# The spatial branch's products as three float16 products of scaled halves, in place of float32 products

## The chip, the cores and the metric

The kernel runs on one core of one Trainium2 chip. The metric is the device time in microseconds (us) of one execution of the whole program; a profiled execution adds a trace of each engine's instructions, whose span runs from the first to the last of them. A core has the engines TensorE (PE, matrix products, with its weight loads PEld), VectorE (DVE), ScalarE (ACT) and GpSimd (POOL), which share the on-chip memory SBUF; products land in the eight banks of PSUM. SyncE (SP), ACT and POOL also issue transfers (DMA).

## The reference

One step of a model layer with three token mixers, for 2048 sample tokens and 128 prompt tokens (2176 together, 17 chunks of 128), with a model width of 1024 and a branch width of 512. From the normalised tokens one input projection gives the columns of branch A (a gated delta rule), branch B (spatial gating in chunks), branch C (a Fourier transform) and the merge gates. The branches are projected, gated, summed and projected again. The change lies in branch B:

```
vn = rmsnorm(v, g_norm).reshape(B, n, CHUNK_B, G_B, CH_B)
vs = jnp.einsum('gpq,bnqgc->bnpgc', w_s, vn) + b_s.T[None, None, :, :, None]
return u * vs.reshape(B, T, W_BR)
```

Here CHUNK_B = 128, G_B = 4 and CH_B = 128: in each chunk of 128 tokens and each of 4 groups of 128 channels, a 128x128 matrix `w_s[g]` mixes the tokens. The root-mean-square is taken over all 512 channels of a token. `u` and the gate `z` of the branch come from the same input projection. All inputs and outputs are float32.

## The kernel before

**Splitting.** Nearly every product is done as three float16 products: an operand is scaled by a power of two, its high half is the float16 of that, and its low half is the float16 of what is left. `mm3` (L168) adds high x high, high x low and low x high in one PSUM bank. `scales` (L183) finds a power of two from a sum of squares: a product with ones adds over the partitions, and three integer operations on DVE make the scale and its inverse. Weights are converted so in `converting` (L203), by an ACT square with a running sum, `scales`, an ACT copy to float16 (L223) and a DVE operation for the low half (L224). The spatial products were an exception: they are float32 (`mm` at L1164).

**Order of the work.** The main line of the program is a sequence of stages: the modulation and the normalised tokens `xh`, `xl`; the columns of branch A with their short convolution (L611); the spatial branch's `v` (L1175); its `u` and `z` (L1207); branch C (L1242); the merges with the gates (L1356); the output projection (L1507). Beside it runs a second line, the delta rule of branch A (`prep`, `base_inverse`, `scan`), as a generator that `pace` (L312) advances a step whenever the main line has done a certain amount of work (`pace.tick`). So both lines are in one program. The tile framework then orders the instructions of each engine ahead of time with a simulated timeline (`schedule_with_timeline_sim=True`, L1572); blocks under `tc.high_priority()` go ahead there. On the chip each engine runs its own queue in that fixed order.

**Around the change.** `wsn`, the four matrices, is loaded at L638 into a buffer of the tag "st" (three buffers). Before the loop TensorE transposes them into a PSUM bank of `ps_x` (two banks) and DVE copies that to `wsT`, float32 (L1156). The loop at L1175 takes the 17 chunks of 128 tokens. For each, TensorE adds 8 x 3 float16 products of 128x512 into a bank of `ps_mm` (three banks); DVE scales it into `vn` (L1184, tag "sg", four buffers); ACT squares it with a sum over the 512 channels (L1187, its output in "st" is not used); DVE and POOL make the reciprocal root (L175, L176). Then `spatial` runs for the chunk before (L1160): four float32 products, stationary `vn`, moving `wsT`, and four DVE operations that multiply by the gain and add the bias (L1166). Results are stored to DRAM up to three chunks later (`vstore`, L1169). Last in the body, DVE multiplies `vn` by the root (L1193), for the next turn's `spatial`, and `pace.tick(5.2)` advances the delta rule.

The stage after it reads the results back by channel group (`vrow`, L1206 and L1212) and multiplies them by `u` straight from PSUM (L1218); `z` goes through a sigmoid on ACT (L1128) and a DVE product (L1130). Both take banks of `ps_mm`.

The delta rule's work beside this stage is the preparation of its chunks (L686: transposes L695 and L728, squares L701, roots L702 and L703, DVE products L743 and L759, halves L747 and L748) and the inverses of 32x32 triangles (L771: the ladder on DVE at L792 and L793, halves at L798 and L799).

Of the kernel before, what the change touches and what calls it, by code (L numbers as in the profile page):

```python
# [11 lines left out]
F16 = mybir.dt.float16  # L12
I32 = mybir.dt.int32
BF16 = mybir.dt.bfloat16
AF = mybir.ActivationFunctionType
ALU = mybir.AluOpType
# [4 lines left out]
P = 128  # L21
# [7 lines left out]
WB = 512  # L29
EPS = 1e-6  # L30
# [5 lines left out]
AD = (0, 2, 4, 6)  # L36
CQ = 545
FS = 4096.0
TBS = [(0, 512), (512, 512), (1024, 512), (1536, 512), (2048, 128)]

_CONSTS = [
# [75 lines left out]
def hybrid_flow_kernel(ctx: ExitStack, tc: tile.TileContext, x_prompt, x_sample, state_delta, c, c_ctx, ln_g, w_ada,  # L117
# [3 lines left out]
    V, A, G, PE, SY = nc.vector, nc.scalar, nc.gpsimd, nc.tensor, nc.sync  # L121
    uid, rot = [0], [0]

    def nm(s):
        uid[0] += 1
        return f"{s}_{uid[0]}"
# [4 lines left out]
    def sb(pl, shape, tag, dt=F32, bufs=None):  # L131
        kw = {} if bufs is None else {"bufs": bufs}
        return pl.tile(list(shape), dt, tag=tag, name=nm(tag), **kw)
# [9 lines left out]
    ep = pool(ctx, "ep", 2)  # L143
# [18 lines left out]
    mhalf = sb(cp, [P, 1], "mhalf")  # L162
    G.memset(mhalf, -0.5)

    def mm(out, l, r, start=True, stop=True):
        PE.matmul(out, l, r, start=start, stop=stop)  # L166

    def mm3(out, l, r, start=True, stop=True):  # L168

        mm(out, l[0], r[0], start, False)  # L170
        mm(out, l[0], r[1], False, False)
        mm(out, l[1], r[0], False, stop)

    def rsqrt(out, ss, mul, w):
        V.tensor_scalar(out, ss, mul, EPS, ALU.mult, ALU.add)  # L175
        G.tensor_tensor(out, out, mhalf.to_broadcast([P, w]), ALU.pow)  # L176
# [6 lines left out]
    def scales(ss, pl, tag, sb16=None):  # L183

        ps = bank(ps_x, [P, 1])
        mm(ps, ones16, widened(ss, pl, tag) if sb16 is None else sb16)
        t = sb(pl, [P, 4], tag)
        V.tensor_copy(t[:, 0:1], ps)
        h = t[:, 3:4].bitcast(I32)
        V.tensor_scalar(h, t[:, 0:1].bitcast(I32), 24, None, ALU.logical_shift_right)  # L190
        V.tensor_scalar(t[:, 1:2].bitcast(I32), h, -8388608.0, 204.0 * 8388608, ALU.mult, ALU.add)
        V.tensor_scalar(t[:, 2:3].bitcast(I32), h, 8388608.0, 50.0 * 8388608, ALU.mult, ALU.add)
        return t[:, 1:2], t[:, 2:3]
# [164 lines left out]
    pc = sb(cp, [P, NPRM], "pc")  # L358
# [9 lines left out]
        V.tensor_copy(pc, pp)  # L368

    convw = lambda j, ct: pc[:, 8 + j * 12 + ct:8 + j * 12 + ct + 1]  # L370
    sgug = lambda g: pc[:, 44 + g:45 + g]
    ong = pc[:, 48:49]


# [22 lines left out]
    for blk in range(8):  # L397
        if blk == XB:
            load_x(*TBS[0])
            columns()  # L400
        ps = bank(ps_d, [2, 256])
        for k0 in range(0, KT, 4):
            st = sb(p0p, [P, 4, 256], "ast", bufs=8)
# [31 lines left out]
    with tc.issue_after(last_ada.ins):  # L435
        read_next()
        read_next()
        load_x(*TBS[1])
        zaw = getw(4)
        bdp = sb(wp, [P, KT, 32], "bdp", F16, bufs=1)  # L440
        bdw = load_w(w_in_[:, C_BD:C_BD + 16], KT, 16, hi=bdp[:, :, 0:16], lo=bdp[:, :, 16:32], tag="d")
    szlate = []
    for ti, (t0, tn) in enumerate(TBS):
        if t0 not in xts:
            load_x(t0, tn)
        g = 0 if t0 < NS else 1
# [10 lines left out]
        for k in range(KT):  # L457
            ps = bank(ps_d, [P, tn])
            for j in range(nt):
                PE.transpose(ps[:, j * P:(j + 1) * P], xt[:, j, k * P:(k + 1) * P], ident)  # L460
            t = sb(p0p, [P, tn], "xm", bufs=3)
# [3 lines left out]
        for g in range(4):  # L465
            ps = bank(ps_d if tn == P and g % 2 else ps_mm, [P, tn])
# [33 lines left out]
    def decays():  # L500
# [14 lines left out]
        for d in range(2):  # L515
            A.activation(beta[:, d], pbv[:, 0, d], AF.Sigmoid, scale=bdw.inv)
        V.tensor_scalar(beta, beta, 1.0 / (FS * FS), None, ALU.mult)
        yield 1
# [40 lines left out]
        A.activation(flat(ed), flat(ed), AF.Exp)  # L559
        V.tensor_scalar(flat(ed), flat(ed), FS, None, ALU.mult)  # L560
        V.tensor_scalar(flat(neg), flat(eg), -1.0 / FS, None, ALU.mult)
        yield 1
# [48 lines left out]
    for ct in range(12):  # L611
        w = getw(1, 2 if ct < 6 else min(4, 15 - ct))
        for half in range(1):
# [3 lines left out]
            G.memset(raw[:, LP - 1:LP], 0.0)  # L617
            for t0, tn in TBS:
                flip[0] ^= 1
                ps = bank(ps_d if flip[0] else ps_mm, [P, tn])  # L620
# [65 lines left out]
    def prep(g, ci, t, nxt, held):  # L686
# [40 lines left out]
        for h in range(H):  # L727
            PE.transpose(ps[:, hs(h)], tok[:, 0, hs(h)], ident)  # L728
        made = A.activation(T[:, 0, :], ps, AF.Copy, scale=FS)
        V.scalar_tensor_tensor(T[:, 1, :], ps, FS, T[:, 0, :], ALU.mult, ALU.subtract)  # L730
        more(2, lambda: rows(2, nxt))
# [8 lines left out]
        for d in range(2):  # L740
# [5 lines left out]
            n16 = sb(d2, [P, 2, WB], "n16", F16, bufs=4)  # L746
            made = A.activation(n16[:, 0, :], n_, AF.Copy, scale=FS)  # L747
            V.scalar_tensor_tensor(n16[:, 1, :], n_, FS, n16[:, 0, :], ALU.mult, ALU.subtract)  # L748
# [373 lines left out]
    def silu_unit(ti, w, out_scale=None):  # L1122
        t0, tn = TBS[ti]
        ps = bank(ps_mm, [P, tn])
# [8 lines left out]
    def gate_unit(n, g, ti, w, src, sg=None, out_scale=None):  # L1133

        t0, tn = TBS[ti]
        own = sg is None
# [11 lines left out]
    bp = pool(bs, "bp", 2)  # L1148
    bsp = sb(bp, [P, 4, P], "bsp", bufs=1)
    SY.dma_start(bsp, b_spatial[0].rearrange("g (o p) -> o g p", o=1).to_broadcast([P, 4, P]))  # L1150
    wsT = sb(bp, [P, 4, P], "wsT", bufs=1)
    vw = getw(4, 3)
    ps = bank(ps_x, [P, 4, P])
    for g in range(4):
        PE.transpose(ps[:, g, :], wsn[:, g, :], ident)
    V.tensor_copy(wsT, ps)  # L1156
    vinv = sb(ep, [P, 4], "vinv", bufs=1)
    for i in range(4):
        V.tensor_copy(vinv[:, i:i + 1], vw[i].inv)
    def spatial(t, vn):  # L1160
        vs = sb(bp, [P, 4, P], "vs", bufs=4)
        ps = bank(ps_x, [P, 4, P])
        for g in range(4):
            mm(ps[:, g, :], vn[:, g, :], wsT[:, g, :])  # L1164
        for g in range(4):
            V.scalar_tensor_tensor(vs[:, g, :], ps[:, g, :], sgug(g), bsp[:, g, :], ALU.mult, ALU.add)  # L1166
        vout.append((t, vs))

    def vstore(made):  # L1169
# [4 lines left out]
    vout, vprev = [], None  # L1174
    for t in range(NCH):  # L1175
        ps = bank(ps_mm, [P, 4, P])
        ts = slice(t * P, (t + 1) * P)
        for k in range(KT):
            mm(ps, xh[:, k, ts], v4[0][:, :, k, :], k == 0, False)
            mm(ps, xh[:, k, ts], v4[1][:, :, k, :], False, False)  # L1180
            mm(ps, xl[:, k, ts], v4[0][:, :, k, :], False, k == KT - 1)
        vn = sb(ep, [P, WB], "sg", bufs=4).rearrange("p (i c) -> p i c", i=4)
        with tc.high_priority():
            V.tensor_tensor(vn, ps, vinv.rearrange("p (i o) -> p i o", o=1).to_broadcast([P, 4, P]), ALU.mult)  # L1184
        sq = sb(ep, [P, WB], "st", bufs=3)
        ss = sb(bp, [P, 1], "vss", bufs=3)
        made = A.activation(sq, vn.rearrange("p i c -> p (i c)"), AF.Square, accum_out=ss)  # L1187
        rsqrt(ss, ss, 1.0 / WB, 1)
        if vprev is not None:
            spatial(*vprev)  # L1190
        if len(vout) > 2:
            vstore(made)
        V.tensor_scalar(vn, vn, ss, None, ALU.mult)  # L1193
        vprev = (t, vn)
        if t == 8:
            SY.dma_start(cf, consts16)
        pace.tick(5.2)
    spatial(*vprev)
    while vout:
        vstore(made)  # L1200
# [6 lines left out]
    for g in range(4):  # L1207
# [5 lines left out]
        for ti, (t0, tn) in enumerate(TBS):  # L1213
            st = vrow[:, t0:t0 + tn]
            ps = bank(ps_mm, [P, tn])
# [26 lines left out]
    for g in range(4):  # L1242
        xw, zw = getw(2, 2)
        for gh in range(1):
# [20 lines left out]
            for q in range(0, NCH, 4):  # L1265
                qn = min(4, NCH - q)
                ps = bank(ps_mm, [P, qn, P])
                for i in range(qn):
                    t = q + i
# [43 lines left out]
            for q4 in range(5):  # L1313
# [8 lines left out]
                if q4 == 2:  # L1322
                    ps = bank(ps_x, [P, P])
# [183 lines left out]
    for i_, t in enumerate(order):  # L1507
# [11 lines left out]
        for i, (c0, c1) in enumerate([(0, 512), (512, 896), (896, D)] if end else [(0, 512), (512, D)]):  # L1519
            cs = slice(c0, c1)  # L1520
            ps = bank(ps_mm, [P, c1 - c0])
# [54 lines left out]
```

## Time and profile before

| what | us |
|---|---|
| timed runs | 2195.5, 2200.12, 2200.22 (median 2200.12) |
| the profiled execution | 2197.38 |
| its span | 2195.6 |
| PE busy in the span | 2122.4 |
| DVE busy | 1311.2 |
| ACT busy | 1013.1 |
| POOL busy | 737.1 |

How to read the profile. Busy time is the union of an engine's instructions; matrix products are pipelined, so their durations overlap and a busy PE isn't at its peak. A row of the timeline gives start, duration, engine, line, operation, what is written and read, shapes and count, and in brackets the idle time of the engine before it with what ended it. A row of the stretches gives the stretch, its length, then for PE, PEld, DVE, ACT and POOL the busy time with the count of instructions, the granted TensorE clock (1.00 is full), the mean share of the DMA engines and GB/s. A row of a line or a tile gives the count, the least, median and greatest duration in ns, and the first and last start in us. A row of the groups gives count, busy us, mean ns, and then the idle time before it and what ended most of it.

### The profile page before, as it was taken

The page shows a single profiled execution, that of the slowest core. Times are in us where ns is not written, and L with a number is a line of the kernel's source. Part 1 is how long each engine was busy: PE and PEld are TensorE (multiplying, and loading weights), DVE is VectorE, ACT ScalarE, POOL GpSimd, SP SyncE. Part 2 cuts the span into 40 slices and gives each one's busy share as a digit, 9 for nine tenths or more (in the row PEclk, how much of TensorE's full clock was granted, in tenths as well). Part 3 has the DMA queues.
Part 4 walks back from the last instruction along what each step waited for, and adds up shares of the span by engine and source line. Part 5 has one row for each costly group of instructions (what it writes and reads, how often), then busy time and mean ns, then how long its engine had stood idle before and what let it go on. Part 6 is the DMA issues. An engine that isn't in the chain of part 4 may idle for free.

```text
span 2195.6 us, 42626 instructions
## 1 busy us (share of the span) xinstructions
PE 2122.4 (97%) x16258; PEld 1218.2 (55%) x16258; DVE 1311.2 (60%) x3141; ACT 1013.1 (46%) x2345; POOL 737.1 (34%) x893
## 2 busy tenths in 40 slices
PE   7999999999999999899899999999999999999998
PEld 3565444455455577777455555555655444444444
DVE  5736845479878697466655555755574544233454
ACT  3544644355555674444544445655553422222332
POOL 1421533223334332443321223345442222122553
PEclk9999999999999999999999999999999999999999
DMA  8434733167777754434645556766665544333542
GB/s 282 143 96 146 266 114 110 61 208 219 239 224 238 213 167 107 119 118 143 217 155 166 167 161 187 239 195 206 204 200 154 166 125 129 119 101 109 183 151 106
DMA packets 304280, 365.11 MB, mean 166 GB/s; under 512 B 39393, under 2 KB 215754, under 8 KB 302026
## 3 DMA queue, kind: packets, MB, share of 16 engines
q1 hardware_dynamic: 251690, 267.38, 40.5%
q0 software_dynamic: 12688, 51.27, 6.5%
q10 hardware_dynamic: 39696, 43.72, 5.9%
q8 instruction: 128, 2.10, 0.4%
q14 instruction: 78, 0.64, 0.1%
HBM read 234.67 MB, written 127.62 MB: 165 GB/s over the span
## 4 chain that ended last, share of the span: by engine, by line
PE 45%; DVE 8%; DMA 7%; ACT 3%; issue 2%; POOL 1%; ACTq 0%; SPq 0%; POOLq 0%; DVEq 0%
PE b L166 45%; DMA st<-br 1%; DMA wst<-in_w_in_dram 1%; DVE XB L792 1%; DVE E L793 1%; DMA ei<-XB 1%; DMA wst<-in_w_branch_dram 1%; DMA sv<-kv 1%; DMA mt<-mrg 1%; DVE wlo L224 1%; DVE o L925 0%; DMA mrg<-mrow 0%; ACT nd L745 0%; DVE sv L980 0%; DVE big L1354 0%
## 5 line engine op out<-in xcount | busy, mean ns | idle before, releaser
L166 PE MATMUL b<-xh,whi 128*128 128x512 f16 (+1 forms) x1920 | 650.2, 347 | 7.4 <-DVE sg L1130 3.4
L166 PE MATMUL b<-xl,whi 128*128 128x512 f16 (+1 forms) x1920 | 650.6, 347 | 0.0
L166 PE MATMUL b<-xh,wlo 128*128 128x512 f16 (+1 forms) x1920 | 649.8, 347 | 0.0
L166 PEld LDWEIGHTS <-whi 128*128 128x128 f16 x3904 | 356.7, 98 | 339.6 <-issue 15.8
L166 PEld LDWEIGHTS <-wlo 128*128 128x128 f16 x1952 | 191.1, 98 | 177.9 <-issue 1.5
L166 PE MATMUL b<-big,bhi 128*128 128x512 f16 (+1 forms) x960 | 251.7, 348 | 5.8 <-ACT big L1353 5.4
L1393 POOL TENSOR_TENSOR mrow<-mrow,sg 128x512 f32<-128x512 f32 (+1 forms) x80 | 96.0, 1201 | 289.0 <-DVE sg L1392 158.5
L166 PE MATMUL b<-big,blo 128*128 128x512 f16 (+1 forms) x480 | 163.7, 348 | 0.0
L1383 ACT ACTIVATE sg<-b,winv 128x512 f32<-128x512 f32 (+1 forms) x120 | 74.1, 618 | 154.0 <-PE b L166 153.6
L166 PEld LDWEIGHTS <-xh 128*128 128x128 f16 x1496 | 118.7, 99 | 35.0 <-DVE yT L1306 3.9
L633 POOL TENSOR_TENSOR cy<-cy,raw 128x545 f32<-128x545 f32 (+1 forms) x48 | 76.6, 1623 | 180.3 <-ACT raw L632 180.3
L166 PEld LDWEIGHTS <-bhi 128*128 128x128 f16 x960 | 87.2, 98 | 77.0 <-ACT big L1353 1.6
L180 DVE CAST wscb<-wss 128x1 bf16<-128x1 f32 x93 | 14.3, 154 | 192.4 <-ACT wlo L214 79.4
L1392 DVE SCALAR_TENSOR_TENSOR sg<-b,binv,sg 128x512 f32<-128x512 f32 (+1 forms) x80 | 53.5, 668 | 101.2 <-PE b L166 91.1
L166 PE MATMUL b<-whi,xh 128*128 128x128 f16 x544 | 95.2, 222 | 5.2 <-DVE yT L1306 3.7
L166 PE MATMUL b<-wlo,xh 128*128 128x128 f16 x544 | 95.2, 222 | 0.0
L166 PE MATMUL b<-whi,xl 128*128 128x128 f16 x544 | 95.1, 222 | 0.0
L166 PE MATMUL b<-wohi,mh 128*128 128x512 f16 (+2 forms) x248 | 91.9, 372 | 1.5 <-ACT mh L1463 1.5
L865 POOL COPY T<-ES 32x256 f16<-32x256 f16 x68 | 28.7, 422 | 191.5 <-DMA ES<-ei 178.2
L166 PE MATMUL b<-wohi,ml 128*128 128x512 f16 (+2 forms) x248 | 91.7, 372 | 0.3 <-DVE ml L1464 0.3
L166 PE MATMUL b<-wolo,mh 128*128 128x512 f16 (+2 forms) x248 | 91.9, 372 | 0.0
L224 DVE SCALAR_TENSOR_TENSOR wlo<-wst,wsc,whi 128x1024 f16<-128x1024 f32 x52 | 72.6, 1399 | 31.2 <-ACT whi L223 30.4
(458 smaller groups left out, 4305.2 us busy)
## 6 DMA issues: line engine op xcount, KB each, us to landing
wst<-in_w_in_dram SPq DMA_DIRECT2D x60, 512.0 KB, 5.9
qkv<-cy POOLq DMA_DIRECT2D x12, 1089.0 KB, 5.2
st<-br SPq DMA_DIRECT2D x48, 256.0 KB, 4.5
mrow<-mrg SPq DMA_DIRECT2D x18, 512.0 KB, 3.5
mrow<-mrg SPq DMA_DIRECT2D x16, 576.0 KB, 3.8
mrg<-mrow POOLq DMA_DIRECT2D x16, 576.0 KB, 3.8
dc<-dec SPq DMA_DIRECT2D x17, 512.0 KB
kq<-qkv SPq DMA_DIRECT2D x34, 256.0 KB, 5.1
```

What stands on the lines that cost most here:

```text
L166: PE.matmul(out, l, r, start=start, stop=stop)
L180: V.tensor_copy(sb16, ss)
L224: V.scalar_tensor_tensor(w.lo, st, s, w.hi, ALU.mult, ALU.subtract)
L633: G.tensor_tensor(y[:, c0:c1], y[:, c0:c1], raw[:, 1 + c0:1 + c1], ALU.mult)
L792: V.tensor_tensor(t3, X3[:, 0:k, k:k + 1].to_broadcast([P, k, n_]), E3[:, k:k + 1, k:32].to_broadcast([P, k, n_]), ALU.mult)
L793: V.tensor_tensor(E3[:, 0:k, k:32], E3[:, 0:k, k:32], t3, ALU.subtract)
L865: G.tensor_copy(T16[rows(a0, b), :, :, b], ES[0:32, :, 2 * a0 + b, :, wT])
L1383: A.activation(sg, ps, AF.Sigmoid, scale=gw.inv)
L1392: V.scalar_tensor_tensor(sg, ps, binv[:, 1:2], sg, ALU.mult, ALU.mult)
L1393: G.tensor_tensor(mr, mr, sg, ALU.add)
```

## The change

The spatial weights are now held as two float16 halves under one scale, which `scales` finds from their sum of squares; its inverse goes into a small tile `vg` with the gains. A chunk's values get a fixed scale of 2048 (`VS`), folded into the reciprocal root's constants; ACT makes the high half from `vn` times the root and DVE the low half, in a buffer of the tag "st", over the square's unused output. `vn` itself is no longer scaled in place. `spatial` calls `mm3` in place of `mm`, and its evictions multiply by `vg` in place of the gain.

```
+VS = 2048.0
...
-    sgug = lambda g: pc[:, 44 + g:45 + g]
...
-    wsT = sb(bp, [P, 4, P], "wsT", bufs=1)
+    wsT = sb(bp, [P, 2, 4, P], "wsT", F16, bufs=1)
     vw = getw(4, 3)
     ps = bank(ps_x, [P, 4, P])
     for g in range(4):
         PE.transpose(ps[:, g, :], wsn[:, g, :], ident)
-    V.tensor_copy(wsT, ps)
+    wss = sb(bp, [P, 1], "vss", bufs=3)
+    A.activation(wsT[:, 1], ps, AF.Square, accum_out=wss)
+    wscale, winv_ = scales(wss, bp, "wssc")
+    A.activation(wsT[:, 0], ps, AF.Copy, scale=wscale)
+    V.scalar_tensor_tensor(wsT[:, 1], ps, wscale, wsT[:, 0], ALU.mult, ALU.subtract)
+    vg = sb(bp, [P, 4], "vg", bufs=1)
+    V.tensor_scalar(vg, pc[:, 44:48], winv_, 1.0 / VS, ALU.mult, ALU.mult)
...
         for g in range(4):
-            mm(ps[:, g, :], vn[:, g, :], wsT[:, g, :])
+            mm3(ps[:, g, :], [vn[:, l, g * P:(g + 1) * P] for l in range(2)], [wsT[:, l, g, :] for l in range(2)])
         for g in range(4):
-            V.scalar_tensor_tensor(vs[:, g, :], ps[:, g, :], sgug(g), bsp[:, g, :], ALU.mult, ALU.add)
+            V.scalar_tensor_tensor(vs[:, g, :], ps[:, g, :], vg[:, g:g + 1], bsp[:, g, :], ALU.mult, ALU.add)
...
-        sq = sb(ep, [P, WB], "st", bufs=3)
+        vn = vn.rearrange("p i c -> p (i c)")
+        v2 = sb(ep, [P, WB], "st", bufs=3).bitcast(F16).rearrange("p (l x) -> p l x", l=2)
         ss = sb(bp, [P, 1], "vss", bufs=3)
-        made = A.activation(sq, vn.rearrange("p i c -> p (i c)"), AF.Square, accum_out=ss)
-        rsqrt(ss, ss, 1.0 / WB, 1)
+        made = A.activation(v2[:, 1], vn, AF.Square, accum_out=ss)
+        V.tensor_scalar(ss, ss, 1.0 / WB / VS ** 2, EPS / VS ** 2, ALU.mult, ALU.add)
+        G.tensor_tensor(ss, ss, mhalf, ALU.pow)
         if vprev is not None:
             spatial(*vprev)
         if len(vout) > 2:
             vstore(made)
-        V.tensor_scalar(vn, vn, ss, None, ALU.mult)
-        vprev = (t, vn)
+        A.activation(v2[:, 0], vn, AF.Copy, scale=ss)
+        V.scalar_tensor_tensor(v2[:, 1], vn, ss, v2[:, 0], ALU.mult, ALU.subtract)
+        vprev = (t, v2)
```

## The prediction, made before the result was known

> **What bounds the kernel now.** First the top of the page, then the busy time by stretches. The change lies in one stage, the loop over 17 token chunks of the spatial branch (from about 445 us to 565 us), so that stage decides.
>
> ```profile
> span 2195.6 us, 42626 instructions
> PE 2122.4 (97%) x16258; PEld 1218.2 (55%) x16258; DVE 1311.2 (60%) x3141; ACT 1013.1 (46%) x2345; POOL 737.1 (34%) x893
> 445.00:505.00 60.00, 58.90 (x385) 36.37 (x384) 48.08 (x151) 31.99 (x106) 18.51 (x26) 1.00 0.77 225
> 505.00:555.00 50.00, 49.81 (x306) 29.27 (x306) 48.16 (x141) 28.15 (x88) 15.09 (x21) 1.00 0.62 195
> ```
>
> The columns of the last two rows are PE, weight loads, DVE, ACT, POOL, then clock and DMA. Over the whole span TensorE is the bound and DVE has room (60%). In this stage it isn't so: from 505 to 555 us DVE is busy 48.16 of 50 us, beside a TensorE that is busy 49.81. It carries the state branch's preparation and its triangular inverses as well. So two engines are full there, and an edit that takes from one and gives to the other must be counted on both.
>
> Next the products themselves, by tile.
>
> ```profile
> L166 PEld LDWEIGHTS b<-wsT,sg x136: 186/192/192, 450.2 to 560.1; 128*128 128x128 f32 x136
> L166 PE MATMUL b<-wsT,sg x136: 272/275/377, 450.4 to 560.2; 128*128 128x128 f32 x136
> L1156 DVE COPY wsT<-b x1: 691/691/691, 443.7 to 443.7; 128x512 f32<-128x512 f32 x1
> ```
>
> There are 17 x 4 = 68 products and 136 instructions: a float32 product runs as two passes. The durations are pipelined latencies; the price is the distance from one start to the next, which the timeline gives.
>
> ```profile
> 460.39 1.05 PE L166 MATMUL b<-wsT,sg 128*128 128x128 f32 x8
> 461.28 0.38 PE L166 MATMUL b<-v4hi,xh 128*128 128x512 f16 x1
> ...
> 463.02 0.78 PE L166 MATMUL b<-T 128*128 128x128 f16 x11
> 463.63 0.72 PE L166 MATMUL b<-q,T 128*128 128x128 f16 x10
> 464.19 0.61 PE L695 MATMUL b<-cst,kq 128*128 128x128 f32 x4
> ```
>
> One chunk's eight passes take 461.28 - 460.39 = 0.89 us, 0.111 each. The state branch has float16 products of the same 128x128x128 size: 11 from 463.02 to 463.63 and 10 to 464.19, 1.17 us for 21, or 0.056 each.
>
> **The change, part by part.**
>
> *Products.* 8 passes of 0.111 become 12 of 0.056: 0.89 - 0.67 = 0.22 us less per chunk, 17 chunks give **-3.8 us on TensorE**. Bounds: 0, if each float16 product waits for its weights as long as a float32 pass does (then 12 x 0.111 = 1.33, and the stage loses 7.5 us instead), to -3.8; I take -3.8, because the rows at 463.02 also change their stationary operand at each product.
>
> *Splitting each chunk.* DVE's scaling at L1193 goes; one ACT copy to float16 and one DVE pass for the low half come. The square that writes float16 instead of float32, the two operations of the reciprocal root and the four evictions stay one for one.
>
> ```profile
> L1193 DVE TENSOR_SCALAR sg<-sg,vss 128x512 f32<-128x512 f32 x17 | 8.5, 500 | 2.3 <-POOL vss L176 2.1
> L720 ACT ACTIVATE q<-qr,qsc x17: 705/707/722, 450.8 to 808.9; 128x512 f16<-128x512 f32 x17
> L747 ACT ACTIVATE n<-n x34: 629/630/632, 468.2 to 833.1; 128x512 f16<-128x512 f32 x34
> L721 DVE SCALAR_TENSOR_TENSOR q<-qr,qsc,q x17: 729/745/750, 451.6 to 812.1; 128x512 f16<-128x512 f32 x17
> L748 DVE SCALAR_TENSOR_TENSOR n<-n,n x34: 670/687/801, 469.9 to 833.9; 128x512 f16<-128x512 f32 x34
> ```
>
> L720 and L721 are the same pair with a scale read per partition, as here; L747 and L748 have a constant scale and give the low end. ACT: +0.71 (0.63 to 0.71) per chunk, 12 us in all; ACT is busy 60.14 of 110 us in the two stretches above, so the sum lies beside other work, and only its place in the chain counts. DVE: 0.745 - 0.500 = +0.25 (0.19 to 0.25) per chunk, **+4.2 us on DVE** (3.2 to 4.2).
>
> *Set-up.* In place of one copy (0.69): an ACT square, a cast, one product with ones, four small DVE operations, an ACT copy and a DVE pass, some 3 us of chain by the rows above, plus one small product for the gains. From the copy's start at 443.7 to the first product at 450.4 TensorE runs chunks that are independent of it; that hides it, even if the first three chunks' squares are ahead of it on ACT. If the cover fails, TensorE waits once, 3 us at most. The transposed weights stay in one of two PSUM banks for these 3 us, and a weight-scale product behind them would wait as long. I take 0 (0 to +3). No DMA is added or moved, and nothing is moved past a queue of SP or POOL. The halves now hold one of three "st" buffers until their products, about one chunk; the old square's output was freed at once. Three buffers at one chunk each do; cost 0, and a square that waits would be one chunk late (6.5 us, once).
>
> *What waits.* The chain from root to product was POOL, DVE, TensorE and becomes POOL, ACT, DVE, TensorE: 0.71 + 0.25 later. Behind the waiting product in TensorE's queue stand the next chunk's 24 products; behind the ACT copy the squares of the preparation; behind the DVE pass the next eviction, on which a PSUM bank depends. What this chain costs already is in the group of the weight loads:
>
> ```profile
> L166 PEld LDWEIGHTS b<-wsT,sg 128*128 128x128 f32 x136 | 17.2, 191 | 3.3 <-DVE sg L1193 1.3 <-DVE vs L1166 0.6
> ```
>
> 1.3 us of TensorE's queue in 17 chunks end on L1193: the products mostly stand late enough. The order on each engine is set ahead by a planner (L1572), which sees the longer chain too. I take +0 (0 to 6 x 0.96 = 5.8, if one chunk in three is exposed in full).
>
> *How the stage ends.* This decides what of the -3.8 comes out. The next stage multiplies by the result read back from DRAM, and its first eviction waits for it.
>
> ```profile
> 554.91 0.13 DVE L175 TENSOR_SCALAR vss<-vss 128x1 f32<-128x1 f32 x1
> 555.68 1.00 POOL L176 TENSOR_TENSOR vss<-vss,mhalf 128x1 f32<-128x1 f32 x1
> 558.03 0.47 DVE L1193 TENSOR_SCALAR sg<-sg,vss 128x512 f32<-128x512 f32 x1
> 559.45 1.06 PE L166 MATMUL b<-wsT,sg 128*128 128x128 f32 x8
> 562.24 0.75 DVE L1130 SCALAR_TENSOR_TENSOR sg<-b,winv,sg 128x512 f32<-128x512 f32 x1 [2.46 <-ACT sg L1128]
> 563.37 1.13 DVE L1166 SCALAR_TENSOR_TENSOR vs<-b,pc,bsp 128x128 f32<-128x128 f32 x4
> 564.53 0.39 ACTq L1172 DMA_DIRECT2D vs<-vs  x1
> L1206 SPq DMA_DIRECT2D vrow<-vs x1: 656/656/656, 570.9 to 570.9; - x1
> 577.43 0.75 DVE L1218 SCALAR_TENSOR_TENSOR vrow<-b,winv,vrow 128x512 f32<-128x512 f32 x1 [1.21 <-DMA vrow<-vs]
> 573.41 0.77 PE L166 MATMUL b<-T 128*128 128x128 f16 x11 [1.45 <-DVE T L730]
> 578.23 0.59 PE L166 MATMUL b<-xh,whi 128*128 128x512 f16 x1 [3.04 <-DVE vrow L1218]
> ```
>
> The last chunk's results are stored at 564.5, read back from 570.9, and used at 577.4; TensorE stands 3.04 us until then. That chain is DVE's, not TensorE's: the root's first operation (554.91) and the scaling (558.03) come out of the stretch where DVE is 96% full. If TensorE finishes its share 3.8 us sooner and the read-back doesn't, the gain is only a longer wait at 575 us. The read-back's shift: the last chunk's longer chain, 0.71 + 0.25 - 0.22 = +0.7; DVE's backlog, 8 chunks x 0.25 = 2.0 in the full stretch against its 1.84 us of idle time, so between 0.2 and 2.0, I take +1.1; and against both a slack of 3.0 us, for the products ended at 560.4 and L1166 started at 563.37, behind L1130, which waited for ACT. The +1.8 thus lies between wholly hidden and wholly exposed; half of the slack holds if L1130 moves with TensorE, so +0.3.
>
> The restart after that wait has a price too.
>
> ```profile
> 572.00:578.00 6.00, 1.78 (x25) 0.96 1.06 389
> 578.00:581.00 3.00, 2.77 (x7) 0.50 0.61 215
> ```
>
> After the 3 us without products the granted clock is 0.50 from 578 to 581 us: 7 products in 3 us where 14 fit at 0.216, 1.5 us lost. With the 0.96 before it (6 x 0.04 / 0.5 = 0.5 us at half) that makes 3.5 us at half clock, most of it after the restart. A longer wait would begin the half clock earlier, and could end it earlier (-1.5, nothing lost any more) or hold it for as long again (+1.5); I take +0.4, since a longer wait is colder.
>
> By the Trainium skill, "TensorE: Matmul & The Clock Gate", Part 1: The HAM clock gate, the clock falls to half after an idle window of about 3.4 us and comes back after a window as long that is busy. The trace agrees with the length (3.5 us above) and halves after a wait of 3.04 us. By that rule a wait made longer by 3.8 us is surely a whole idle window, and a whole busy one must follow at half clock: an estimate from the page is 1.7 us lost in place of 1.5, so +0.2 where the sum has +0.4.
>
> **Sum.** -3.8 on TensorE, given back at 575 us (+3.8); read-back +0.3; restart +0.4: **+0.7 us**. The profiled execution took 2197.4 us (span 2195.6 and 1.8 around it), so 2198.1 for it; the three timed runs have the median 2200.1, 2.7 above the profiled one, and I put the sum on that: **2200.8**. A difference under 0.3% (6.6 us) is about what a measurement of this kernel can't tell from none.
>
> **Rivals.**
>
> *The saving comes through.* If DVE catches up (7.24 us busy in the ten after 555) and the read-back moves forward with TensorE, all of -3.8 stays: 2196.3. Against it speaks the 96%.
>
> *Faster.* The planner lays the queues anew, and the waits around the read-back close: 3.8 + 1.45 + 3.04 + the lost clock (7 x 0.216 = 1.5) = -9.8: 2190.3. For it: the products at 573.41 show that preparation work, which needs no row, can stand there. Against it: nothing in the change shortens the two DMA trips.
>
> *Slower: the longer chain and the full DVE set the pace.* DVE's +4.2 and its set-up (+1.0) come out whole, since it has 1.84 us spare in 50, and the exposed chunks add 5.8: +11: 2211.1. It decides from the point at which DVE's added work in the stretch (2.0 us) passes its idle time (1.84), so it is near; against it, the three PSUM banks let TensorE run ahead two chunks, and before 505 us DVE has 12 us spare. A new order of the later stages works in the same direction or the other: they hold these waits of TensorE,
>
> ```profile
> 571.00:640.00 69.00, 63.88 (x403) 35.26 (x402) 60.52 (x146) 40.22 (x121) 27.19 (x34) 0.98 0.72 238
> 640.00:760.00 120.00, 115.50 (x738) 63.99 (x737) 89.45 (x211) 67.00 (x203) 44.84 (x53) 1.00 0.73 221
> 760.00:900.00 140.00, 130.71 (x1662) 105.52 (x1660) 114.82 (x317) 73.86 (x197) 40.44 (x61) 0.98 0.46 133
> ```
>
> 5.1 + 4.5 + 9.3 = 18.9 us, of which a third either way is 6 us.
>
> *It doesn't do what it says.* The float16 products are bound by their weight loads, 0.111 each: +7.5: 2207.6.
>
> **Chances.** Forecast 0.32; saving comes through 0.16; faster 0.22; slower 0.27; products dearer 0.03. The first two lie within 0.3%: faster 0.22, same 0.48, slower 0.30. The likeliest case alone spans 2197 to 2205; as cases of both signs hold half of the chance, the range reaches past their points, 2188 to 2214, with about one in ten left out on each side.
>
> **What would show it.** Products: 204 float16 matmuls from the halves, a chunk's twelve in 0.67 us. DVE: 17 passes of 0.745 in place of L1193's, and 505 to 555 us at 98% or more. The end: TensorE's wait for the row read back longer than 3.04 us, and the first product after it no earlier than 577 us. If that product comes at 574 us, the saving came through. Wrong from the start would be a chunk of twelve products at 0.89 us or more, or a PE wait for the weights' halves near 450 us; and if the time moves by more than the stage's end does, the cause lies in the order of later work, which this sum doesn't hold.

## The result, and the profile after

The changed kernel took 2191.61 us (median of 8 runs, 2187.5 to 2196.13), the kernel before 2199.39 us on the same chip (8 runs). The ratio is **0.9962, with an interval of 0.9948 to 0.9975**: faster by some 8 us. Two more measurements of the same changed kernel gave 0.9978 [0.9965, 0.9991] and 0.9968 [0.9957, 0.998], so the three together stand for about 0.997, 6 to 7 us. The forecast was 2200.8, no change. The profiled execution took 2190.95 us, its span 2189.2.

The page of the changed kernel, and its busy time in the two stretches in which DVE was full before:

```profile
span 2189.2 us, 42789 instructions
PE 2120.1 (97%) x16327; PEld 1212.7 (55%) x16327; DVE 1325.3 (61%) x3147; ACT 1025.6 (47%) x2365; POOL 722.4 (33%) x893
```

```profile
445.00:505.00 60.00, 59.42 (x428) 34.82 (x426) 49.53 (x152) 40.89 (x123) 17.91 (x26) 1.00 0.74 217
505.00:555.00 50.00, 49.65 (x366) 29.29 (x364) 49.10 (x143) 29.62 (x92) 16.47 (x22) 1.00 0.70 216
```

DVE is fuller than before in the second one (49.10 of 50 us, it was 48.16), as forecast. The rows of the tile `wsT` (the products, and the first and last operation of the set-up), and from the groups between 445 and 600 us the low half's pass and the weight loads of the halves:

```profile
L167 PE MATMUL b<-wsT,st x204: 217/219/230, 458.3 to 550.3; 128*128 128x128 f16 x102
L1157 ACT ACTIVATE wsT<-b x1: 598/598/598, 446.0 to 446.0; 128x512 f16<-128x512 f32 x1
L1160 DVE SCALAR_TENSOR_TENSOR wsT<-b,wssc,wsT x1: 751/751/751, 453.0 to 453.0; 128x512 f16<-128x512 f32 x1
```

```profile
L167 PEld LDWEIGHTS <-st 128*128 128x128 f16 x204 | 13.2, 98 | 4.4 <-ACT st L1201 0.6
L1202 DVE SCALAR_TENSOR_TENSOR st<-sg,vss,st 128x512 f16<-128x512 f32 x17 | 12.6, 747 | 1.2 <-ACT st L1201 1.1
```

The set-up takes 7.8 us from its first operation to the end of its last (446.0 to 453.0 and 0.75), not 3, but TensorE doesn't stand for it (59.42 of 60 us busy). DVE waits only 1.1 us in all 17 chunks for ACT's new copy. One chunk's twelve products, in the timeline of TensorE:

```profile
464.47 0.83 PE L167 MATMUL b<-wsT,st 128*128 128x128 f16 x12
465.14 0.83 PE L167 MATMUL b<-q,T 128*128 128x128 f16 x12
```

From start to start that is 0.67 us, as forecast. Then the end of the stage, which decided the forecast (the last chunk's evictions, its store, the read-back, and the first use of it):

```profile
552.36 1.12 DVE L1172 SCALAR_TENSOR_TENSOR vs<-b,vg,bsp 128x128 f32<-128x128 f32 x4
553.51 0.38 ACTq L1178 DMA_DIRECT2D vs<-vs  x1
556.01 0.33 SPq L1215 DMA_DIRECT2D vrow<-vs  x1
561.63 0.75 DVE L1227 SCALAR_TENSOR_TENSOR vrow<-b,winv,vrow 128x512 f32<-128x512 f32 x1 [1.56 <-DMA vrow<-vs]
```

The store stands at 553.51, it was at 564.53; the first use at 561.63, it was at 577.43. TensorE's wait of 3.04 us for the row, and the 1.45 us ahead of it, are gone. What made room on DVE, as far as the rows show: the planner laid the state branch's triangular inverse later. Of its 62 steps on DVE (L792 and L793) all stood in the chunk loop before, from the first eviction of V to the last, and 39 stand there now. In the kernel before, and then in the changed one, ACT's high halves of the finished inverse:

```profile
547.36 2.94 ACT L798 ACTIVATE XB<-E 128x1024 f16<-128x1024 f32 x2 [3.31 <-DVE E L793]
```

```profile
568.14 1.06 ACT L798 ACTIVATE XB<-E 128x1024 f16<-128x1024 f32 x1 [2.59 <-DVE E L793]
569.11 2.00 ACT L798 ACTIVATE XB<-E 128x1024 f16<-128x1024 f32 x1
```

The inverse was done ahead of the last chunk and is now done behind it, in the next stage. There other waits of TensorE have grown, above all one for the gate `z` (first row before, second after):

```profile
661.00 0.38 PE L166 MATMUL b<-xh,whi 128*128 128x512 f16 x1 [2.76 <-DVE sg L1130]
```

```profile
658.10 0.38 PE L167 MATMUL b<-xh,whi 128*128 128x512 f16 x1 [4.38 <-DVE sg L1130]
```

What this comes to is read from two stretches that begin and end with the same instructions in every kernel: from the first eviction of V to the last (the chunk loop), and from there to the last product with `u` (the next stage). Their bounds, the starts of these rows, for the kernel before and then the changed one:

```profile
L1184 DVE TENSOR_TENSOR sg<-b,vinv x17: 677/684/692, 433.5 to 550.1; 128x512 f32<-128x512 f32 x17
L1218 DVE SCALAR_TENSOR_TENSOR vrow<-b,winv,vrow x20: 336/744/752, 577.4 to 766.5; 128x512 f32<-128x512 f32 x16, 128x128 f32<-128x128 f32 x4
```

```profile
L1190 DVE TENSOR_TENSOR sg<-b,vinv x17: 680/684/692, 435.5 to 543.9; 128x512 f32<-128x512 f32 x17
L1227 DVE SCALAR_TENSOR_TENSOR vrow<-b,winv,vrow x20: 338/742/752, 561.6 to 765.4; 128x512 f32<-128x512 f32 x16, 128x128 f32<-128x128 f32 x4
```

And the stretches between them, with their sums:

```profile
433.50:550.10 116.60, 115.31 (x711) 68.20 (x709) 95.14 (x291) 61.36 (x190) 36.85 (x49) 1.00 0.66 201
550.10:766.50 216.40, 206.78 (x1351) 116.28 (x1350) 171.12 (x410) 121.67 (x371) 80.73 (x99) 0.99 0.74 229
sum 333.00, PE 322.08 PEld 184.49 DVE 266.25 ACT 183.03 POOL 117.58; mean PE 161.04 PEld 92.24 DVE 133.13 ACT 91.52 POOL 58.79
```

```profile
435.50:543.90 108.40, 107.47 (x750) 62.04 (x748) 89.88 (x266) 69.48 (x207) 37.27 (x49) 1.00 0.71 215
543.90:765.40 221.50, 211.03 (x1379) 118.28 (x1377) 180.93 (x442) 124.68 (x371) 80.86 (x99) 0.98 0.72 224
sum 329.90, PE 318.49 PEld 180.32 DVE 270.81 ACT 194.15 POOL 118.13; mean PE 159.25 PEld 90.16 DVE 135.40 ACT 97.08 POOL 59.06
```

The loop became 8.2 us shorter and the stage behind it 5.1 us longer; both together 3.1 us shorter. TensorE is busy 3.59 us less (322.08 to 318.49) and idle 0.49 more (10.92 to 11.41). So in this trace TensorE's work fell by what the products save, and its waits were dealt out anew with nearly the same sum. In a second trace of the changed kernel it is much the same (318.27 busy, 11.83 idle); a third, with 333.0 us for both stages, comes up below. From branch C on, the order of the instructions is the same in both kernels.

### The profile page after: what moved, and what is told of

It is laid out like the page before. It is cut to its first block, busy times and chain, and to the rows that moved or that the text cites. A ratio compares the mean times of both kernels' runs of the same rounds, so it can differ in the third digit from the quotient of the medians.

```text
span 2189.2 us, 42789 instructions
## 1 busy us (share of the span) xinstructions
PE 2120.1 (97%) x16327; PEld 1212.7 (55%) x16327; DVE 1325.3 (61%) x3147; ACT 1025.6 (47%) x2365; POOL 722.4 (33%) x893
## 4 chain that ended last, share of the span: by engine, by line
PE 49%; DVE 7%; DMA 5%; ACT 3%; issue 2%; POOL 1%; ACTq 0%; SPq 0%; POOLq 0%; DVEq 0%
PE b L167 49%; DMA st<-br 2%; DMA wst<-in_w_in_dram 1%; DVE XB L792 1%; DVE E L793 1%; DMA wst<-in_w_branch_dram 1%; ACT nd L745 0%; DVE big L1363 0%; DVE wlo L225 0%; DMA ei<-XB 0%; PE b L1056 0%; DMA wst<-mrg 0%; ACT big L1362 0%; DMA XB<-nd 0%; ACT whi L224 0%
## 5 line engine op out<-in xcount | busy, mean ns | idle before, releaser
L633 POOL TENSOR_TENSOR cy<-cy,raw 128x545 f32<-128x545 f32 (+1 forms) x48 | 66.4, 1409 | 186.5 <-ACT raw L632 186.5
```

What stands on the lines that cost most here:

```text
L633: G.tensor_tensor(y[:, c0:c1], y[:, c0:c1], raw[:, 1 + c0:1 + c1], ALU.mult)
```

## The experiments

Two theories stood at first. **Matrix time counts**: what TensorE saves comes out at the end. **Order decides**: the planner's order of the two stages, laid anew for any edit, makes the difference, whatever the products cost. In the first expectations these are called theory A and theory B. In the table, the loop and both stages are those of the rows above, from one profiled execution each; the ratio is to the kernel before on the same chip, with its interval.

| kernel | us | ratio | loop | both stages |
|---|---|---|---|---|
| before (first trace; again) | 2196.59 (again) | 0.9994 [0.9982, 1.0005] | 116.6; 116.2 | 333.0; 332.6 |
| changed (three times) | 2191.61; 2193.34; 2193.08 | 0.9962; 0.9978; 0.9968 (intervals above) | 108.4; 107.6; 107.6 | 329.9; 330.1; 333.0 |
| chain alone | 2204.16 | 1.0038 [1.0025, 1.0051] | 113.7 | 334.9 |
| set-up alone | 2206.62 | 1.0049 [1.0035, 1.0064] | 112.0 | 334.7 |
| products twice | 2199.03 | 1.0012 [1.0002, 1.0023] | 119.5 | 341.2 |
| one product of three | 2183.61 | 0.9945 [0.9931, 0.9958] | 102.3 | 323.2 |
| all but the products (twice) | 2190.25; 2193.37 | 0.9972 [0.996, 0.9985]; 0.9966 [0.9954, 0.9978] | 111.4; 111.0 | 329.0; 329.0 |
| another tick | 2209.32 | 1.0051 [1.0035, 1.0067] | 113.0 | 340.4 |
| float32 products, changed kernel's order | 2197.42 | 0.9995 [0.9984, 1.0007] | 109.9 | 334.0 |
| changed, order of "all but the products" (twice) | 2188.46; 2190.12 | 0.9959 [0.9943, 0.9975]; 0.9958 [0.9943, 0.9973] | 110.5; 111.2 | 327.0; 329.2 |
| before, changed kernel's order | 2193.43 | 0.9982 [0.9972, 0.9991] | 108.7 | 331.9 |
| changed, order of before (19 us lost ahead of the loop) | 2229.96 | 1.0143 [1.0123, 1.0163] | 128.2 | 345.8 |
| changed, order of before in the loop | 2216.8 | 1.008 [1.0067, 1.0092] | 131.2 | 354.4 |

A single trace is worth less than it looks: the changed kernel's three have 329.9, 330.1 and 333.0 for one program. In the third TensorE is idle 11.83 us, as in the second, but busy 321.17: it was at half clock for 3.6 us longer, which costs up to 1.8, as the last section works out, and 20 more of its instructions stand ahead of the last product with `u`.

**One part at a time.** The chain alone, in the kernel before, with float32 products:

```
-        V.tensor_scalar(vn, vn, ss, None, ALU.mult)
-        vprev = (t, vn)
+        vf = vn.rearrange("p i c -> p (i c)")
+        A.activation(sq, vf, AF.Copy, scale=ss)
+        V.scalar_tensor_tensor(sq, vf, zc, sq, ALU.mult, ALU.add)
+        vprev = (t, sq.rearrange("p (i c) -> p i c", i=4))
```

> The kernel before, with the changed kernel's chain and engine load but its own float32 products: after the root, ACT writes the scaled chunk (0.7 us) and a DVE pass follows it (0.75 us in place of 0.50), in the buffer of the square. The result is the reference's. Theory A (TensorE bounds the stage, DVE has room because its ladder can run later): -2 to +2 us against before, and the changed kernel is 4 us or more below it. Theory B (the gain is the new order of the queues, not the products): some us off before in either direction, by the order that it gets; the changed kernel need not be below it. The prediction's slower rival (DVE and the longer chain set the pace): +5 to +11.

The set-up alone, with float32 weights (`wsT` goes through `scales`, an ACT copy and a DVE pass, and the gains through `vg`):

```
-    V.tensor_copy(wsT, ps)
+    A.activation(wsT, ps, AF.Square, accum_out=wss)
+    wscale, winv_ = scales(wss, bp, "wssc")
+    A.activation(wsT, ps, AF.Copy, scale=wscale)
+    V.scalar_tensor_tensor(wsT, ps, zc, wsT, ALU.mult, ALU.add)
+    V.tensor_scalar(vg, pc[:, 44:48], winv_, None, ALU.mult)
```

> The kernel before with the set-up of the changed one alone: the spatial weights go through square, scale, an ACT copy and a DVE pass, all in float32, and the gains take the inverse scale. Loop and products are those of before; the result is the reference's. Theory A: 0 to +3 us, since TensorE has other chunks to do until 450 us. Theory B: as likely -5 as +5, since the order of the later queues is laid anew.

They cost 8 and 11 us by their medians. But both together, which is the change without its float16 products (the lines are against the changed kernel; its halves become float32 too):

```
-            mm3(ps[:, g, :], [vn[:, l, g * P:(g + 1) * P] for l in range(2)], [wsT[:, l, g, :] for l in range(2)])
+            mm(ps[:, g, :], vn[:, g, :], wsT[:, g, :])
```

> The changed kernel in all but the products: set-up and chain are the changed kernel's (square, scale, ACT copy, DVE pass, at the same places and lengths), but they carry float32 and the four products of a chunk are float32 as before. The result is the reference's. It differs from the changed kernel by 8 passes of 0.111 us in place of 12 of 0.056 per chunk. Theory A (matrix time counts one for one): 3.8 us above the changed kernel, so about -4 against before, and at the end of the u and z stage 3.8 us later than the changed kernel. Theory B (orders of the queues decide): the set-up alone was +11 and the chain alone +8 against before, so this is 5 to 15 above before, and 10 or more above the changed kernel.

gained as much as the whole change (0.9972, and 0.9966 when measured again), with the products still float32. Two losses that add up to a gain can't be prices of instructions. That spoke for the order, and so did a kernel that has no new instruction at all, but asks the planner for another pace of the state branch:

```
-        pace.tick(5.2)
+        pace.tick(5.0)
```

> The kernel before, with the second line of work advanced by 5.0 in place of 5.2 per chunk of this loop: no work is added or taken, two steps or so of the state branch move behind the loop and the queues of the stage are laid anew. Theory A: within 2 us of before. Theory B: 4 us or more off before, in either direction.

It lost 12 us (1.0051). **The matrix time by itself**, on the changed kernel: each product twice with the gains halved, and only high x high, which leaves the low halves out of the result.

```
-    V.tensor_scalar(vg, pc[:, 44:48], winv_, 1.0 / VS, ALU.mult, ALU.mult)
+    V.tensor_scalar(vg, pc[:, 44:48], winv_, 0.5 / VS, ALU.mult, ALU.mult)
...
-            mm3(ps[:, g, :], [vn[:, l, g * P:(g + 1) * P] for l in range(2)], [wsT[:, l, g, :] for l in range(2)])
+            for r_ in range(2):
+                mm3(ps[:, g, :], [vn[:, l, g * P:(g + 1) * P] for l in range(2)], [wsT[:, l, g, :] for l in range(2)], r_ == 0, r_ == 1)
```

> The changed kernel with every spatial product done twice into the same bank and the gains halved, so that the result is the same: TensorE gets 17 x 12 x 0.056 = 11.4 us more, DVE and ACT nothing. Theory A: 11 us above the changed kernel, so about +3 against before. Theory B and the prediction (the read-back by way of DVE ends the stage): 0 to 4 above the changed kernel, -4 to -8 against before.

```
-            mm3(ps[:, g, :], [vn[:, l, g * P:(g + 1) * P] for l in range(2)], [wsT[:, l, g, :] for l in range(2)])
+            mm(ps[:, g, :], vn[:, 0, g * P:(g + 1) * P], wsT[:, 0, g, :])
```

> The changed kernel with one product (high by high) in place of three, so that the low halves are made and not used and the result has float16's precision there: TensorE loses another 17 x 8 x 0.056 = 7.6 us, DVE and ACT nothing. Theory A: 7 us below the changed kernel, about -15 against before. Theory B and the prediction: within 3 us of the changed kernel.

Both stages became 11.3 us longer for 11.4 us of added products (341.2 against 329.9), and 6.7 shorter for 7.6 removed. The whole times, against the three of the changed kernel, say 3.4 to 5.0 thousandths more (7 to 11 us) and 1.7 to 3.3 less (4 to 7 us). That spoke for the matrix time, but in all these kernels the planner had laid the order too. The rest of the kernels therefore hold it: the order of the instructions is taken from one kernel and forced on another, for the engines named, by a dependence of each on the one before it. The two kernels in the changed kernel's order hold DVE, ACT and POOL; the changed kernel in the order of "all but the products" holds every engine.

```
+    for e, text in _ORDER.items():
+        at = np.cumsum(np.frombuffer(zlib.decompress(base64.b85decode(text)), np.int32))
+        for a, b in zip(at[:-1], at[1:]):
+            tc.add_manual_dep(made[e][int(b)], made[e][int(a)].name, dep, reason="order")
```

**The same order, other products.** Float32 products in the order of the changed kernel, and the changed kernel in the order laid for float32 products:

> All of the change except the products, which stay float32, with the order of the instructions of DVE, ACT and POOL written out by hand as the changed kernel has it; TensorE and the DMA queue of SP are left to the planner. 'Order decides': as the changed kernel (ratios so far 0.9962 and 0.9978), 0.997 give or take 0.0013, and the u and z stage ends 2 to 5 us earlier than in the kernel before. 'Matrix time counts': 3.8 us more than the changed kernel, 0.9987, and the stage ends within 1 us of the kernel before.

> The changed kernel with every engine's order written out by hand as the planner laid it for the same kernel with float32 products (measured 0.9972, stage end 4.0 us earlier than before). Only the matrix time differs from that run, 11.4 us in place of 15.1. 'Order decides': 0.9972 give or take 0.0013, stage end at -4.0 give or take 1. 'Matrix time counts': 3.8 us less, 0.9955, stage end at -7.8.

In the first order the difference is 1.7 to 3.3 thousandths (0.9995 against 0.9962 to 0.9978), 4 to 7 us. It isn't the products' alone: TensorE's order was left to the planner there, and from the first spatial products on, near 459 us, to the start of branch C it differs from the changed kernel's. The second order is held on every engine, and the difference is about one thousandth (0.9959 and 0.9958 against 0.9972 and 0.9966), 2 to 3 us, with intervals that overlap. The forecast's 3.8 lies between the pairs. The two-stage sums, first with float32 and then with float16 products, in the order laid for float32:

```profile
sum 329.00, PE 320.78 PEld 184.56 DVE 268.62 ACT 194.70 POOL 118.10; mean PE 160.39 PEld 92.28 DVE 134.31 ACT 97.35 POOL 59.05
```

```profile
sum 327.00, PE 317.20 PEld 180.31 DVE 268.73 ACT 194.91 POOL 117.94; mean PE 158.60 PEld 90.16 DVE 134.37 ACT 97.45 POOL 58.97
```

TensorE is busy 3.58 us less there. That the work is saved is thus seen; that the whole time falls by it rests on the products done twice (7 to 11 us, where "order decides" expected 0 to 4) and once (4 to 7, where it expected at most 3) and on both pairs, which all go the same way. So "order decides" hardly stands alone, though the one pair with every engine held lies too close together to show it. The two kernels of that pair were run again side by side:

> Float32 products with the rest of the change, in the planner's own order, once more: 0.9972 give or take 0.0013, stage end at -4.0 give or take 0.5.

> The changed work in the order of the kernel with float32 products, once more. 'Matrix time counts' in a given order: 2 to 4 us under the run with float32 products, and as much under the changed kernel, so 0.995 to 0.9965, stage end at -6. 'Order decides' alone: as the run with float32 products, 0.9972.

The medians were 3.3 us apart, but the second trace with float16 products had 329.2 for both stages, level with 329.0: one trace can't show a difference of 2 or 3 us. The changed work in that order is, by its ratios, the fastest of the kernels that compute the whole result; its intervals overlap those of the changed kernel.

**The same work, another order.** The same instructions with float32 products took 0.9972 and 0.9966 in one order and 0.9995 in the other: 5 to 6 us from the order alone. And the kernel before, without any new instruction, in the changed kernel's order on DVE, ACT and POOL (its scaling writes the buffer of the square in place of its own):

> The kernel before (float32 products, DVE's scaling of the values, which writes another buffer of the tag st in place of its own), with the order of DVE, ACT and POOL written out by hand as in the changed kernel; none of the new work is in it. 'Order decides': most of the gain without any of the change, 0.997 give or take 0.0015, the u and z stage ends 3 to 5 us earlier. 'Matrix time counts', or the new work is needed for the gain: 1.000 give or take 0.0015, stage end within 1 us of the kernel before.

It gained 4 us (0.9982 [0.9972, 0.9991]), just within what "order decides" expected, though its two stages are only 1.1 us shorter (331.9). With the other pair and the kernel with another tick, "matrix time counts" falls as a theory that stands alone. Its last store and the first use of the row read back (the last start of the first row, the first start of the second):

```profile
L1172 ACTq DMA_DIRECT2D vs<-vs x17: 366/377/380, 460.2 to 552.8; - x17
L1218 DVE SCALAR_TENSOR_TENSOR vrow<-b,winv,vrow x20: 336/744/751, 562.1 to 766.2; 128x512 f32<-128x512 f32 x16, 128x128 f32<-128x128 f32 x4
```

So the order alone brings the store from 564.5 to 552.8 and the first use from 577.4 to 562.1, and TensorE has no wait for the row in this kernel. But its wait for `z` is 4.6 us, near the 4.38 of the changed kernel; it was 2.76. Against this kernel the one with float32 products, set-up and chain in the same order is 0.0013 slower, 3 us; the intervals overlap, so a price of the added work is likely and not shown. Last, the reverse, on which the forecast was built: the changed work in the order of the kernel before.

> The changed kernel's work with the order of TensorE, DVE and POOL written out by hand as in the kernel before (the added instructions stand behind the one that precedes them in the program). This is what the prediction assumed. 'Order decides', and the prediction's own sum: +0.7 us on 2197, ratio 1.0003, within 0.998 and 1.002, the u and z stage ends within 2 us of the kernel before, and TensorE's wait for the row read back is 3 us or longer. 'Matrix time counts': -3.8 us, 0.9983. If the longer chain is exposed in this order: up to +11 us, 1.005.

It was 1.0143, far beyond every expectation, 14 us more than the next run shows without the set-up's part. The first eviction of V came 19 us late (452.4 us, it was 433.5): the set-up's operations stood on TensorE and DVE ahead of their data, with everything else behind them. TensorE waited 17.84 us at the weight scale's product for DVE, and DVE 11.10 us for ACT's square of the weights. With the changed kernel's own order up to the first spatial product, and the old one from there:

> As the run before it that had the changed work in the order of the kernel before (1.0143; its set-up alone cost 19 us there, since the weight scale's operations stood on DVE ahead of their data), but with the changed kernel's own order on TensorE and DVE up to the first spatial product, and the order of the kernel before from there. ACT and POOL are left to the planner. If the set-up was the whole of that loss: 1.000 give or take 0.002, the last eviction of V and the stage's end within 2 us of the kernel before. If the longer chain through ACT is exposed when the order isn't laid for it: +10 to +13 us at the last eviction of V and at the stage's end, 1.005 or 1.006. 'Matrix time counts' alone: -3.8 us, 0.998.

It still took 1.008 [1.0067, 1.0092], 17 us more than the kernel before, with a loop of 131.2 us in place of 116.6, and more than the 1.005 or 1.006 expected of an exposed chain. The groups between 445 and 600 us show why, and the first of the stretches:

```profile
L1202 DVE SCALAR_TENSOR_TENSOR st<-sg,vss,st 128x512 f16<-128x512 f32 x17 | 12.7, 751 | 11.7 <-ACT st L1201 11.7
L167 PEld LDWEIGHTS <-st 128*128 128x128 f16 x204 | 13.6, 103 | 13.6 <-issue 4.6 <-DVE st L1202 4.4 <-ACT st L1201 2.5
```

```profile
445.00:505.00 60.00, 51.33 (x350) 30.13 (x348) 42.48 (x135) 35.42 (x106) 14.89 (x21) 0.94 0.59 174
```

DVE, at the old place of the scaling, waits 11.7 us for ACT's copy, ten times the 1.1 of the changed kernel; the weight loads of the halves wait 13.6 where they waited 4.4; TensorE is busy 51.33 of 60 us. In this kernel ACT and POOL were left to the planner, so their part isn't held, and how much of the loss is theirs stays open.

The changed kernel was run twice more as the measure for the others, the kernel before once:

> The changed kernel again, for its place beside the others of this call and for a second trace: -5 to -11 against before. If its trace again gains 3 us by the end of the u and z stage and 5 us more behind it, the later part is of the kernel; if the later part moves by some us from the first trace, it is that one execution's.

> The changed kernel once more, beside the next two on the same chip. Both theories: 0.997 give or take 0.001 and the u and z stage ends 3 us before that of the kernel before; it is the measure for the other two.

> The kernel before again, as a second trace: within 2 us of itself in time; stage by stage within 1 us of the first trace if differences of some us between traces are the kernels', 3 us or more off somewhere if they are those of one execution.

## Why the prediction was wrong, by its own steps

**Products, right.** Twelve in 0.67 us, and TensorE's busy time in the two stages fell by 3.59 us for the 3.8 forecast. (The case against which the forecast names a bound of 0, products as dear as float32 passes, is +7.5 by its own sum.)

**DVE's added work, right.** L1202 is busy 12.6 us, 4.1 more than L1193's 8.5, and DVE is 98% full from 505 to 555 us (49.10 of 50).

**Set-up, right in that TensorE didn't wait for it, wrong in length.** The chain was 7.8 us, not 3, and the first product started 22.8 us behind the first eviction of V (458.3 less 435.5), where it was 16.9 (450.4 less 433.5). TensorE had other work. In the old order it cost 19 us, far over the forecast's bound of +3.

**The longer chain at +0, right by one of its two reasons.** The forecast gave two: that the products mostly stand late enough in the old order, and that the planner sees the longer chain too. The first doesn't bear the 0, nor the bound of 5.8: with the old order on TensorE and DVE the loop is 14.6 us longer (131.2 against 116.6). The second fits the changed kernel, where DVE waits 1.1 us for the copy. The rival "slower: the longer chain and the full DVE set the pace" described what happens in the order on which the rest of the forecast was worked out.

**How the stage ends: the step that failed.** The forecast read from the chain at 554.91 to 578.23 that a full DVE sets the read-back, and gave the saving back there (+3.8, read-back +0.3, restart +0.4). The reading of that trace was sound for its order, but it took DVE's work ahead of the last chunk as fixed. Part of that was the inverse, which has no part in the read-back (its steps are 20.9 of DVE's 95.1 us in the loop before, 13.8 of 89.9 now), and the planner moved its end behind the loop. That it was this move and no other that made the room is read from the rows and wasn't tested by itself. The last store came 11 us earlier, and TensorE had no wait for the row, where a longer one than 3.04 us was forecast. That the order does this and not the new work is shown by the kernel before in the changed order: its store is at 552.8 too, and it has no such wait. So the +3.8 was not given back there: in the first two traces both stages are 3.1 and 2.9 us shorter than in the first trace of the kernel before, with TensorE's idle time 0.5 and 0.9 longer.

**The restart, not where it was forecast, and dearer.** The stretch behind the read-back has full clock now, while half clock appears behind the longer wait for `z`:

```profile
555.00:571.00 16.00, 16.00 (x101) 8.98 (x100) 13.17 (x34) 9.82 (x27) 4.72 (x6) 1.00 0.99 344
658.10:661.50 3.40, 3.40 (x10) 1.29 (x10) 2.27 (x5) 3.40 (x16) 3.23 (x4) 0.58 0.63 214
```

Between 597 and 607 us there is as much again (a granted clock of 0.83 over 10 us: 10 x 0.17 / 0.5 = 3.4 us at half clock). So the two stages have 6.7 us at half clock, with the 3.3 of the last section, where the kernel before had 3.5: up to 1.6 us more lost, for the +0.4 of the sum. The reason given for that +0.4, that a longer wait is colder, no run shows: behind a wait of 4.38 us the clock was 0.58 over 3.4 us, behind one of 3.04 it was 0.50 over 3.

**The rivals.** The time fell between two of them: "the saving comes through" (-3.8) and "faster: the planner lays the queues anew" (-9.8). Their mechanisms both took part. The first is seen in TensorE's busy time. Of the second, the two waits did close (1.45 and 3.04), but others grew, so that their sum didn't. The forecast named that case and put its chance at 0.22, with an objection that answers another question: that nothing in the change shortens the DMA trips. They needn't be shorter, only earlier.

**What stays open.** The medians gained 4 to 8 us and the two stages 3.1 in the first trace (0 in the third). From branch C on the order is the same in both kernels, so no instruction moved there explains the rest, and the traces lay it to their scatter: from the last product with `u` to the end the kernel before took 1429.1 and 1426.2 us in its two traces, the changed kernel 1423.8, 1427.1 and 1426.8 in its three. Nor is the whole gain in the traces, since two of the changed kernel's three profiled executions were slow ones of their runs (2196.51 us with a median of 2193.34, 2195.15 with 2193.08). It can't be said how much of the gain is order and how much products: the order alone gave 4 us to the kernel before, the products 2 to 7 in the two comparisons, one of them with TensorE's order not held, the added work may have taken 3 back, and each of these has an interval of 2 us or more.

## What to carry to other kernels

Where a planner orders the queues, a forecast made in the old order is a forecast for a kernel that won't exist: the same work in two orders differed by 5 to 6 us, and the changed work with the old order in the loop lost 17. So before a saving is given back at a wait, ask what fills the engine that the wait is for, and whether that work could stand elsewhere; if it has no part in the wait, the planner may move it. And to price an edit of a few us, hold the order and compare; the trials that changed one part and let the planner lay the rest gave two losses whose sum was a gain.

## What the runs showed of the hardware

The granted clock after a wait of TensorE was not the same for all waits of about 3 us. In the kernel before, the wait of 3.04 us was followed by 0.50, but the one of 2.76 us at 661 us by full clock (in a second trace of that kernel the wait at this place was 3.20 us, and the clock full again):

```profile
661.00:664.00 3.00, 3.00 (x14) 1.36 (x14) 2.05 (x4) 3.00 (x14) 2.87 (x3) 1.00 0.85 296
```

In the changed kernel the wait of 4.38 us at the same place brought 0.58 for 3.4 us. Two executions of that kernel differ there, the first trace and then the third, each over 15 us around this restart:

```profile
655.00:670.00 15.00, 11.90 (x52) 5.47 (x52) 7.61 (x19) 7.27 (x28) 5.80 (x8) 0.89 0.89 291
```

```profile
653.00:668.00 15.00, 11.50 (x43) 4.92 (x43) 6.35 (x13) 7.27 (x28) 5.79 (x8) 0.77 0.94 303
```

Worked out as time at half clock that is 3.3 us (15 x 0.11 / 0.5) in the one and 6.9 us (15 x 0.23 / 0.5) in the other, so one program can lose up to 1.8 us more in one execution than in another. The kernel before shows it too: from 900 to 910 us, around a restart that waits for DVE, its first trace was granted 0.66 after a wait of 3.68 us and its second 1.00 after one of 3.46. The Trainium skill, "TensorE: Matmul & The Clock Gate", Part 1: The HAM clock gate, gives a window of about 3.4 us that runs freely, so that the length of the cold stretch differs from run to run; the 3.3 and 6.9 us of the changed kernel agree with one such window and with two.
